# A two-block transformer forward pass on one core: neighbourhood heads in tiles of 128 queries with a shared turn of edge weights, and a last norm by square root

## The chip, the core and the metric

The kernel runs on one core of a Trainium2 chip. Five engines work from queues of their own: TensorE (PE in the profile, its weight loads PEld), VectorE (DVE), ScalarE (ACT), GpSimd (POOL) and SyncE (SP), which here only issues DMAs; ACT and POOL issue a few as well. The metric is device time in microseconds of one execution. Lower is better, and versions are compared by the median of several runs on the same chip.

## What is computed

The input is x, 256 tokens of width 1024, and two memories of 256 tokens. It passes through two blocks, all in float32. The first block has an even layer (global attention with rotary positions, window attention with a bias and a sink, memory attention, a gate) and an odd layer (neighbourhood attention with 16 heads of width 64, memory attention, a gate). The second block has a mixer (dilated attention and a short convolution), attention to a second memory, a squared-ReLU MLP of width 4096, and a last norm. The parts that matter here:

```python
def rmsnorm(x, g):
    y = xf * lax.rsqrt(jnp.mean(xf * xf, axis=-1, keepdims=True) + EPS)
    return y * g

def neighborhood_attn(q, k, v, rpb):      # a grid of 4 rows of 64 columns
    colmask = (col[None, :] >= cs[:, None]) & (col[None, :] < cs[:, None] + NA_COLS)
    def one(r):                           # the queries of one grid row
        s = einsum('bqhd,bikhd->bhqik', qblk, kblk) * scale + bias
        s = where(colmask[:, None, :], s, -inf)
        p = softmax(s.reshape(B, H, GRID_W, kr * GRID_W), axis=-1)
        return einsum('bhqik,bikhd->bqhd', p, vblk)
```

A query in grid column c sees 16 columns of all four rows: `cs = clip(c - 8, 0, 48)`. The output of the odd layer is multiplied by silu(gate) and projected; the second block ends with `rmsnorm(x, g_final_2)` after the MLP.

## The kernel before

**Precision.** A float32 operand is split into a high and a low part of type float32r (`split`, `hilo`): ACT writes the high part, DVE the rest. A projection is then three products, high-high, high-low and low-high, which accumulate in PSUM. Weights arrive by SP's DMAs in pieces of 1024 KB (tile `raw`, three buffers), are split into `wh` and `wl` (four buffers each) and multiplied; `wide` yields the pieces of a wide weight, and its `step` says how many k tiles of 128 rows one load holds.

**Order.** Nothing is issued while the program is built. Every operation is recorded by `Plan.record` (line 85) with its dependencies, and `Plan.solve` (line 262) orders all of them at once with a list scheduler: each engine takes, of the operations that are ready, the one with the smallest position in the program. The durations for that come from a cost model, `Plan.cost` (line 133). The order is then fixed and issued from line 286, which is why all instructions bear that line. Background work is queued by `later`, and `pace` lets a step of it in after every few matmuls of a projection (`RATE`); `flush` runs what is left of one tag. So the steps of attention heads lie between the matmuls of projections. Tiles of one tag share a number of buffers: `p` has `PB` = 4, `y` has `YB` = 5, `pp` has `PH` = 4, the large slots `SLOTS` = 24; PSUM has four banks tagged `at` and four tagged `mm`.

**The odd layer.** Its norm is done in `norm_later`, and `turns` transposes the result with TensorE. Here the tokens are put into the order of grid columns: token position = 4 * column + row, so that a query's neighbours lie close together (`by_column`). ACT and DVE do that when they read PSUM, through a strided view. Two groups of eight neighbourhood heads follow (`c0` and `c1`, loop at line 1253): keys, queries and values are projected, then `near_heads` (line 969) queues the steps of the heads.

**near_heads.** In column order, 128 queries see at most 160 keys (`SPAN`): queries 0 to 127 the keys 0 to 159, queries 128 to 255 the keys 96 to 255. `first` computes, for a head, the scores of both query tiles, adds the bias with DVE (which also finds the maximum), takes the exponential on ACT with its sum, and then copies, scaled by 1/sum, a part of 128 keys for each block of 64 queries: four operations on 64 partitions each, from key 0 or key 32 of the 160. Either DVE or ACT may do one (`scaled`, the planner chooses). `second` transposes the two 128x128 squares of a head on TensorE, and after both heads of a pair splits them into high and low (tile `pp`). `third` multiplies, for each of the four 64-query blocks b, a stationary value tile `v[b]` with the high and low weights of that block (128 moving columns), adds the high and low halves of the result with ACT and DVE and hands it to `gated`. The four value tiles hold the keys from 0, 32, 96 and 128 on (`NEAR`). The middle two are put together by POOL's DMAs from the outer two. `steps` (line 920) queues these: `second` of a head comes `LAG[0]` = 2 heads behind `first`, `third` of a pair one more behind. Behind a group's steps, `layer_odd` runs other projections and, after `flush`, the output projection (`out_proj`) of that group.

**The MLP.** It goes by slices of 512 hidden columns, `up` then `down`; the last `down_last` (line 1439) also does the last norm: sums of squares `ms` on ACT, their sum with EPS on DVE, the power -1/2 on POOL (line 1475), then scaling by DVE and ACT and the stores.

Of the kernel before, what the change touches and what calls it, by code (L numbers as in the profile page):

```python
# [16 lines left out]
P = 128  # L17
# [11 lines left out]
NEAR, SPAN = (0, 32, 96, 128), 160  # L29


class Plan:
# [100 lines left out]
    def cost(self, engine, method, args, kwargs, outs, ins):  # L133

        if method == "dma_start":
            o = outs[0]
            nbytes = 4 * math.prod(o.shape)
            return (1040.0 if engine == "gpsimd" else 50.0), 950.0, nbytes
        n = math.prod(outs[0].shape[1:])
        sbuf = not any(self.mine(v) and self.tiles[v.tensor.name]["pool"].space == bass.MemoryType.PSUM for v in ins)  # L140
        col = kwargs.get("bias") is not None or isinstance(kwargs.get("scale"), bass.AP)
        accum = kwargs.get("accum_out") is not None
        if engine == "tensor":
# [166 lines left out]
class Kernel:  # L310
# [347 lines left out]

    def turns(self, tag, halves, key, by_column=False):


        nc = self.nc
        rows, cols = (lambda v: v.rearrange("p (r c) -> p r c", c=COLS)), (lambda v: v.rearrange("p (c r) -> p r c", c=COLS))
        if not by_column:
            rows = cols = lambda v: v
# [303 lines left out]
    def near_heads(self, tag, gi, qs, ks, po, out, before):  # L969
# [4 lines left out]
        v = [self.slot([P, 4, 2, 2, 64], "vp") for _ in range(4)]  # L974
        for k, d in ((0, 0), (1, 3)):
            flat = v[d].rearrange("p r e l c -> p r (e l c)")
            h = bass.AP(flat.tensor, flat.offset, [list(flat.ap[0]), [256, 4], [192, 2], [1, 64]])
            l = bass.AP(flat.tensor, flat.offset + 64, [list(flat.ap[0]), [256, 4], [64, 2], [1, 64]])
# [5 lines left out]
        es, ps, ws = {}, {}, {}  # L984
        before()

        def first(h):
            r, e = divmod(h, 2)
            if e == 0:
# [5 lines left out]
                ps[r] = self.work("p", [P, 2, 2, P], PB)  # L995
            w, bias = ps[r][:, e], es.pop(h)
            st = self.work("st", [P, 8], 8)
            nmax, ssum = st[:, 0:2], st[:, 2:4]
            i, j = divmod(h, 4)
            sc = self.scores_stacked(qs[i][:, j, :], ks[i][0][:, j, :], ks[i][1][:, j, :], ((0, SPAN), (S - SPAN, SPAN)))  # L1000
            p = self.work("p", [P, 2, SPAN], PB)
# [12 lines left out]
        def second(h):  # L1014
            r, e = divmod(h, 2)
            if e == 0:
                ws[r] = self.psum("at", [P, 2, 2, P])
            pt = ws[r]
            for t in range(2):
                nc.tensor.transpose(pt[:, e, t, :], ps[r][:, e, t, :], self.ident)  # L1020
            if e == 1:
                w = self.work("pp", [P, 2, 2, 2, P], PH, F32R)
                self.hilo(w[:, 0], w[:, 1], pt)
                ws[r] = w.rearrange("p l e t (b q) -> p l e (t b) q", b=2)

        def third(r):
            w = ws.pop(r)
            u = self.work("y", [P, S], YB)
            o = self.work("y", [P, S], YB)
            blocks = lambda t: t.rearrange("p (b q) -> p b q", b=4)  # L1030
            for e in range(2):
                pv = self.psum("at", [P, 4, 2, 64])
# [4 lines left out]
                nc.scalar.activation(blocks(u[own]), pv[other, :, 0, :], AF.Copy)  # L1037
                nc.vector.tensor_tensor(blocks(u[own]), pv[own, :, 0, :], blocks(u[own]), ALU.add)
                nc.vector.tensor_tensor(blocks(o[own]), pv[own, :, 1, :], blocks(u[own]), ALU.add)
            out(r, o)  # L1040

        self.steps(tag, first, second, third, 8, 2)
# [348 lines left out]
    def mlp(self, ms):  # L1391
# [94 lines left out]
        def down(s, t):  # L1486
            for c in range(2):
                self.proj_n(self.wide(a["w_down_2"], 512 * s, 4, 512 * c), 4, 512, lambda l, k: t[l][:, k, :],
# [4 lines left out]
        for s in range(NS - 1):  # L1493
            t2 = up(s + 1)
# [37 lines left out]
YB = 5  # L1532
# [91 lines left out]
```

## Time and profile before

| | us |
|---|---|
| runs, median (lowest to highest of 3) | 774.47 (773.76 to 774.75) |
| the profiled execution | 772.73 |
| its span, first to last instruction | 770.8 |
| mean granted TensorE clock, share of full | 0.998 |

The span is a little shorter than the profiled execution's own time, because the latter includes what lies before the first and behind the last instruction. Stages in us from the span's start: the even layer to about 195, the odd layer's norm and projections, the neighbourhood heads of the first group from about 265 to 325 and of the second to 391, the mixer to 505, attention to the second memory to 590, the MLP to the end. The page first gives the busy time of each engine; other views give instructions in order of time, groups of equal instructions, and who waited for whom. In the timeline a row gives start and duration in us, engine, operation, tiles (out<-in), shape and count, and in brackets the idle time before it and what ended it; rows of groups give count, busy us, mean ns of one, and idle time before.

### The profile page before, as it was taken

How to read it: one execution, taken by the hardware profiler on the slowest of the kernel's cores; microseconds unless marked ns; L12 is line 12 of the kernel's file. 1: busy time of each engine (PE TensorE's matmuls, PEld its weight loads, DVE VectorE, ACT ScalarE, POOL GpSimd, SP SyncE). 2: the span in 40 equal slices, each digit the busy share in tenths (PEclk: the TensorE clock that was granted, in tenths of full speed). 3: DMA queues.
4: the chain of work that ended last, by engine and by line, in shares of the span. 5: the costliest groups of instructions: out<-in, count | busy, mean ns of one | idle time of the engine just before them, and what ended most of it. 6: DMA issues, size and time to landing. Idle time of an engine off the chain costs nothing.

```text
span 770.8 us, 11844 instructions
## 1 busy us (share of the span) xinstructions
PE 757.9 (98%) x4338; PEld 658.5 (85%) x4338; DVE 621.2 (81%) x1167; ACT 526.9 (68%) x1035; POOL 54.1 (7%) x90
## 2 busy tenths in 40 slices
PE   9999999999999999999999999999999999999996
PEld 7898888888888888788888888889988888888885
DVE  5999998998889889989998879887777665555565
ACT  5777986876679677766777778655656765555562
POOL 2240010000002201110001100100000000000000
PEclk9999999999999999999999999999999999999999
DMA  9893555454568975886356944375335665656541
GB/s 316 279 274 110 164 172 186 162 165 164 162 201 246 274 213 156 222 265 192 120 178 188 245 158 134 137 227 184 137 117 157 212 179 168 204 175 208 173 155 54
DMA packets 109785, 143.28 MB, mean 186 GB/s; under 512 B 3872, under 2 KB 80736, under 8 KB 109728
## 3 DMA queue, kind: packets, MB, share of 16 engines
q1 hardware_dynamic: 103184, 131.09, 52.4%
q0 software_dynamic: 6112, 11.01, 6.1%
q8 instruction: 34, 0.56, 0.3%
q10 hardware_dynamic: 432, 0.43, 0.2%
q14 instruction: 23, 0.19, 0.1%
HBM read 135.70 MB, written 1.05 MB: 177 GB/s over the span
## 4 chain that ended last, share of the span: by engine, by line
PE 79%; DVE 13%; DMA 3%; ACT 2%; issue 2%; SPq 1%; POOL 0%; POOLq 0%; DVEq 0%; ACTq 0%
PE t_mm L286 59%; PE t_at L286 20%; DVE t_wl L286 4%; DVE t_y L286 2%; DMA t_memT<-in_mem_t_dram 1%; DVE t_p L286 1%; DMA t_raw<-in_w_in_even_dram 1%; DVE t_x L286 1%; DMA t_xT<-in_x_t_dram 1%; DVE t_pp L286 1%; DVE t_st L286 1%; DVE t_sum L286 1%; ACT t_p L286 1%; SPq L286 1%; ACT t_wh L286 1%
## 5 line engine op out<-in xcount | busy, mean ns | idle before, releaser
L286 DVE TENSOR_TENSOR t_wl<-t_raw,t_wh 128x1024 fp32r<-128x1024 f32 (+2 forms) x238 | 287.8, 1214 | 63.6 <-ACT t_wh L286 60.7
L286 ACT ACTIVATE t_wh<-t_raw 128x1024 fp32r<-128x1024 f32 (+2 forms) x238 | 249.5, 1054 | 73.4 <-PE t_mm L286 56.0
L286 PE MATMUL t_mm<-t_mT,t_wh 128*128 128x512 f32 x496 | 180.4, 402 | 0.0
L286 PE MATMUL t_mm<-t_mT,t_wl 128*128 128x256 f32 x496 | 132.1, 285 | 0.0
L286 PE MATMUL t_mm<-t_wh,t_yh 128*128 128x512 f32 (+1 forms) x288 | 113.6, 394 | 0.0
L286 PE MATMUL t_mm<-t_wl,t_yh 128*128 128x512 f32 (+1 forms) x288 | 112.9, 392 | 0.0
L286 PE MATMUL t_mm<-t_wh,t_yl 128*128 128x512 f32 (+1 forms) x288 | 112.2, 392 | 0.0
L286 PEld LDWEIGHTS t_mm<-t_mT,t_wh 128*128 128x128 f32 x496 | 91.2, 188 | 13.8
L286 PEld LDWEIGHTS t_mm<-t_mT,t_wl 128*128 128x128 f32 x496 | 93.3, 189 | 6.4
L286 PE MATMUL t_at<-t_mT,t_wh 128*128 128x512 f32 x240 | 85.8, 395 | 0.0
L286 ACT COPY t_sum<-t_mm 128x256 f32<-128x256 f32 x90 | 33.3, 370 | 46.7 <-PE t_mm L286 45.9
L286 PE MATMUL t_mm<-t_wh,t_gh 128*128 128x256 f32 (+2 forms) x256 | 64.1, 334 | 0.0
L286 PEld LDWEIGHTS t_mm<-t_wl,t_yh 128*128 128x128 f32 x288 | 54.1, 188 | 11.0
L286 PEld LDWEIGHTS t_mm<-t_wh,t_yl 128*128 128x128 f32 x288 | 54.0, 188 | 11.0 <-DVE t_yl L286 0.2
L286 PEld LDWEIGHTS t_mm<-t_wh,t_yh 128*128 128x128 f32 x288 | 54.2, 188 | 10.7 <-ACT t_yh L286 0.4
L286 PE MATMUL t_at<-t_mT,t_wl 128*128 128x256 f32 x240 | 62.6, 280 | 0.0
L286 ACT ACTIVATE t_p<-t_p,t_st 128x256 f32<-128x256 f32 (+3 forms) x119 | 52.1, 454 | 11.5 <-DVE t_st L286 11.2
L286 PEld LDWEIGHTS t_at<-t_mT,t_wh 128*128 128x128 f32 x240 | 44.4, 188 | 8.2 <-issue 0.2
L286 PEld LDWEIGHTS t_at<-t_mT,t_wl 128*128 128x128 f32 x240 | 45.2, 188 | 3.6
L286 PE MATMUL t_mm<-t_hT,t_wh 128*128 128x512 f32 (+1 forms) x160 | 48.1, 356 | 0.0
L286 DVE TENSOR_TENSOR t_sum<-t_mm,t_sum 128x256 f32<-128x256 f32 x90 | 38.0, 422 | 11.9 <-ACT t_sum L286 10.6
L286 PEld LDWEIGHTS t_mm<-t_wh,t_gh 128*128 128x128 f32 x256 | 44.1, 191 | 3.6 <-ACT t_wh L286 0.4
(183 smaller groups left out, 1328.4 us busy)
## 6 DMA issues: line engine op xcount, KB each, us to landing
t_raw<-in_w_in_odd_dram SPq DMA_DIRECT2D x20, 1024.0 KB, 5.2
t_raw<-in_w_up_dram SPq DMA_DIRECT2D x16, 1024.0 KB, 5.8
t_raw<-in_w_down_dram SPq DMA_DIRECT2D x16, 1024.0 KB, 5.2
t_raw<-in_w_in_dram SPq DMA_DIRECT2D x12, 1024.0 KB, 5.4
t_raw<-in_w_in_even_dram SPq DMA_DIRECT2D x10, 1024.0 KB, 5.1
t_raw<-in_w_mem_kv_dram SPq DMA_DIRECT2D x8, 1024.0 KB, 5.1
t_raw<-in_w_out_even_dram SPq DMA_DIRECT2D x6, 1024.0 KB, 5.0
t_raw<-in_w_out_odd_dram SPq DMA_DIRECT2D x6, 1024.0 KB, 5.0
```

Source lines behind the costliest of these rows:

```text
L286: f(*[self.real(v) for v in args], **{k: self.real(v) for k, v in kwargs.items()})
```

## The change

- **near_heads** works by tiles of 128 queries. Each tile has its own 128 keys (queries 0 to 127: keys 0 to 127; the others: keys 128 to 255) and 32 edge keys (128 to 159, or 96 to 127). There are two value tiles, and one small tile `edges` with edge keys of the values, which POOL's DMAs place at partitions 32 j for head j of a four.
- `first` scales the own part in place, full width, and writes the edge part, 32 keys for each of two tiles, into a tile shared by four heads (`rests`).
- `second` transposes the own parts of a pair. A new step `turn_rest` transposes the edge parts of four heads at once, keeps the 64 queries of each tile that see edge keys, and splits them.
- `third` has, for each query tile, one matmul over 128 keys (256 moving columns) and one over 32 edge keys (128 moving columns) that adds to half of it.
- The steps are queued by a list of positions instead of `steps`; `third` of both pairs of four heads follows their `turn_rest`. `YB` is 6.
- **turns**: with `by_column`, the transposes write PSUM in column order, and ACT and DVE read it contiguously.
- **Last norm**: square root on ACT and reciprocal on DVE instead of the power on POOL; for the second token tile the last sum goes in as the root's bias. A root on two values is taken early in the MLP, in the pass s = 1.
- **Loads**: the down weights of the last two slices come in halves of 512 KB.
- **Cost model**: a matmul costs at least 111 ns (before, (at least 128 columns)/2.4 + 13.3 = 66.6); ACT work on fewer than 128 partitions costs 100 ns more, DVE work 84 ns more.

```diff
-            return 108.0 if method == "transpose" else max(n * slow, 128) / 2.4 + 13.3, 0.0, 0
+            return 108.0 if method == "transpose" else max(n * slow / 2.4 + 13.3, 111.0), 0.0, 0
-            return n / 1.2 + (93 if sbuf else 51) + 94 * col + 93 * accum + self.table, 0.0, 0
+            return n / 1.2 + (93 if sbuf else 51) + 94 * col + 93 * accum + 100 * half + self.table, 0.0, 0
-            return n / 0.96 + 68 + 62 * ptr + 82 * accum, 0.0, 0
+            return n / 0.96 + 68 + 62 * ptr + 82 * accum + 84 * half, 0.0, 0
...
+    def by_column(v, t):
+        return v.rearrange("p (c r) -> p r c", c=COLS)[:, 2 * t:2 * t + 2, :]
...
-                    nc.tensor.transpose(pt[:, j, t * P:(t + 1) * P], halves[c][:, t, k * P:(k + 1) * P], self.ident)
+                    nc.tensor.transpose(place(pt[:, j, :], t), halves[c][:, t, k * P:(k + 1) * P], self.ident)
-                h, l, v = cols(f(0, 4 * c + k)), cols(f(1, 4 * c + k)), rows(pt[:, j, :])
+                h, l, v = f(0, 4 * c + k), f(1, 4 * c + k), pt[:, j, :]
...
-        for d in (1, 2):
-            n = P - NEAR[d]
-            nc.gpsimd.dma_start(v[d][:n], v[0][NEAR[d]:])
-            nc.gpsimd.dma_start(v[d][n:], v[3][:P - n])
+        edges = self.slot([P, 2, 2, P], "ve")
+        for t, at in enumerate(AT):
+            for j in range(4):
+                if EDGE * j != at:
+                    nc.gpsimd.dma_start(edges[EDGE * j:EDGE * j + EDGE, t], v[1 - t][at:at + EDGE, :, j]
+                                        .rearrange("p i l c -> p i (l c)"))
...
+            edge = bass.AP(p.tensor, p.offset + P, [list(p.ap[0]), [EDGE, 2], [1, EDGE]])
+            nc.vector.tensor_tensor(rests[i][:, :, j, :], edge, ssum.unsqueeze(2).to_broadcast([P, 2, EDGE]), ALU.mult)
             for t in range(2):
-                for b in range(2):
-                    rows, k0 = slice(64 * b, 64 * b + 64), 32 * b
-                    self.scaled(w[rows, t, :], p[rows, t, k0:k0 + P], ssum[rows, t:t + 1])
+                main = p[:, t, EDGE * t:EDGE * t + P]
+                self.scaled(main, main, ssum[:, t:t + 1])
...
+        def turn_rest(i):
+            rest = rests[i]
+            pt = self.psum("at", [P, 2, P])
             for t in range(2):
+                nc.tensor.transpose(pt[:, t, :], rest[:, t].rearrange("p j k -> p (j k)"), self.ident)
+            w = rests[i] = self.work("y", [P, 2, 2, 64], YB, F32R)
+            seen = bass.AP(pt.tensor, pt.offset + 64, [list(pt.ap[0]), [64, 2], [1, 64]])
+            self.hilo(w[:, 0], w[:, 1], seen)
...
-                for b in range(4):
-                    nc.tensor.matmul(pv[:, b], v[b][:, r, e].rearrange("p l c -> p (l c)"), w[:, :, e, b, :],
-                                     start=True, stop=True)
+                for t in range(2):
+                    main, edge = stationary(h, t)
+                    qs_ = slice(64 - 64 * t, 128 - 64 * t)
+                    nc.tensor.matmul(pv[:, t], main, w[:, :, e, t, :], start=True, stop=False)
+                    nc.tensor.matmul(pv[:, t, :, qs_], edge, rest[rows, :, t, :], start=False, stop=True)
...
-        self.steps(tag, first, second, third, 8, 2)
+        steps = [(h, lambda h=h: first(h)) for h in range(8)]
+        steps += [(2 * r + 1.2 + LAG[0], lambda r=r: second(r)) for r in range(4)]
+        steps += [(4 * i + 3.3 + LAG[0], lambda i=i: turn_rest(i)) for i in range(2)]
+        steps += [(4 * (r // 2) + r % 2 + 3.4 + LAG[0] + LAG[1], lambda r=r: third(r)) for r in range(4)]
...
-            parts = [list(self.wide(a["w_down_2"], 512 * s, 4, 512 * c)) for c in range(2)]
+            parts = [list(self.wide(a["w_down_2"], 512 * s, 4, 512 * c, step=2)) for c in range(2)]
...
                 if tt == 1:
-                    nc.vector.tensor_tensor(r, r, ms[:, 2:3], ALU.add)
-                nc.gpsimd.tensor_tensor(r, r, self.mhalf[:, :1], ALU.pow)
+                    nc.scalar.activation(r, ms[:, 2:3], AF.Sqrt, bias=r)
+                else:
+                    nc.scalar.activation(r, r, AF.Sqrt)
+                nc.vector.reciprocal(r, r)
...
+            if s == 1:
+                nc.table = 1300.0
+                nc.scalar.activation(self.work("st", [P, 8], 8)[:, :2], r2, AF.Sqrt)
+                nc.table = 0.0
...
-YB = 5
+YB = 6
```

More of the change, by code (lines that the diff above doesn't have):

```diff
@@ L142, in cost @@
         accum = kwargs.get("accum_out") is not None
+        half = outs[0].shape[0] < P
         if engine == "tensor":
@@ L657, in square_sum @@
                          "op1": ALU.add, "accum_out": ms}))
+    @staticmethod
+    def by_column(v, t):
+        return v.rearrange("p (c r) -> p r c", c=COLS)[:, 2 * t:2 * t + 2, :]
     def turns(self, tag, halves, key, by_column=False):
         nc = self.nc
[L663 to L665 removed]
+        place = self.by_column if by_column else lambda v, t: v[:, t * P:(t + 1) * P]
         f = Halves(lambda: self.slot([P, 2, 2, S], "mT"))
@@ L994, in first @@
                 es[h], es[h + 1] = near[:, 0], near[:, 1]
-                ps[r] = self.work("p", [P, 2, 2, P], PB)
-            w, bias = ps[r][:, e], es.pop(h)
+            if j == 0:
+                rests[i] = self.work("y", [P, 2, 4, EDGE], YB)
+            bias = es.pop(h)
             st = self.work("st", [P, 8], 8)
             nmax, ssum = st[:, 0:2], st[:, 2:4]
-            i, j = divmod(h, 4)
             sc = self.scores_stacked(qs[i][:, j, :], ks[i][0][:, j, :], ks[i][1][:, j, :], ((0, SPAN), (S - SPAN, SPAN)))
-            p = self.work("p", [P, 2, SPAN], PB)
+            p = ps[h] = self.work("p", [P, 2, SPAN], PB)
             for t in range(2):
@@ new lines, in second @@
+        def second(r):
+            pt = self.psum("at", [P, 2, 2, P])
+            for e in range(2):
+                p = ps.pop(2 * r + e)
+                for t in range(2):
+                    nc.tensor.transpose(pt[:, e, t, :], p[:, t, EDGE * t:EDGE * t + P], self.ident)
+            w = ws[r] = self.work("pp", [P, 2, 2, 2, P], PH, F32R)
+            self.hilo(w[:, 0], w[:, 1], pt)
+        def turn_rest(i):
+            rest = rests[i]
+            pt = self.psum("at", [P, 2, P])
+            for t in range(2):
+                nc.tensor.transpose(pt[:, t, :], rest[:, t].rearrange("p j k -> p (j k)"), self.ident)
+            w = rests[i] = self.work("y", [P, 2, 2, 64], YB, F32R)
+            seen = bass.AP(pt.tensor, pt.offset + 64, [list(pt.ap[0]), [64, 2], [1, 64]])
+            self.hilo(w[:, 0], w[:, 1], seen)
@@ L1036, in third @@
                 own, other = slice(64 * e, 64 * e + 64), slice(64 - 64 * e, 128 - 64 * e)
-                nc.scalar.activation(blocks(u[own]), pv[other, :, 0, :], AF.Copy)
-                nc.vector.tensor_tensor(blocks(u[own]), pv[own, :, 0, :], blocks(u[own]), ALU.add)
-                nc.vector.tensor_tensor(blocks(o[own]), pv[own, :, 1, :], blocks(u[own]), ALU.add)
+                nc.scalar.activation(halves(u[own]), pv[other, :, 0, :], AF.Copy)
+                nc.vector.tensor_tensor(halves(u[own]), pv[own, :, 0, :], halves(u[own]), ALU.add)
@@ L1045, in rope @@
+        for _, step in sorted(steps, key=lambda s: s[0]):
+            self.later(tag, step)
     def rope(self, tag, po, n, i, rx):
```

47 lines of the change are left out of this document (24 added, 23 removed).

## The prediction, made before the changed kernel ran

> **What bounds the kernel now.** First the page's busy line and the chain that ended last.
>
> ```profile
> span 770.8 us, 11844 instructions
> PE 757.9 (98%) x4338; PEld 658.5 (85%) x4338; DVE 621.2 (81%) x1167; ACT 526.9 (68%) x1035; POOL 54.1 (7%) x90
> PE 79%; DVE 13%; DMA 3%; ACT 2%; issue 2%; SPq 1%; POOL 0%; POOLq 0%; DVEq 0%; ACTq 0%
> ```
>
> TensorE is the bound: matmuls cover 757.9 of 770.8 us. So time can fall in three ways only: fewer matmul slots, fewer waits of TensorE inside, or a shorter tail behind the last matmul. Work taken from VectorE (DVE) or ScalarE (ACT) counts only where TensorE waits for it. Next the busy time of the first neighbourhood stage, and what the weight loads (PEld) waited for between 255 and 410 us, where both groups of neighbourhood heads lie.
>
> ```profile
> 255.00:325.00 70.00, 68.83 (x387) 59.05 (x387) 63.51 (x139) 51.46 (x106) 10.79 (x18) 1.00 0.75 212
> ...
> PEld t_at L286 <- ACT t_sum L286: 2.0, 3, 1.4
> PEld t_at L286 <- ACT t_wh L286: 0.8, 2, 0.6
> PEld t_at L286 <- DVE t_xg L286: 0.7, 1, 0.7
> ...
> PEld t_at L286 <- ACT t_p L286: 0.3, 1, 0.3
> ```
>
> The columns of the first row are length, then busy us of PE, PEld, DVE, ACT and POOL, then the granted clock (1.00) and DMA. The t_xg wait belongs to the norm behind the stage; the other six, 3.1 us, stand in front of the neighbourhood's product of weights and values (t_at<-t_pp,t_vp). The longest, in the timeline:
>
> ```profile
> 318.86 1.39 DVE L286 TENSOR_TENSOR t_ks<-t_sum,t_ks 64x512 fp32r<-64x512 f32 x2
> ...
> 320.96 0.68 DVE L286 TENSOR_TENSOR t_pp<-t_at,t_pp 128x512 fp32r<-128x512 f32 x1
> ...
> 321.76 0.97 PEld L286 LDWEIGHTS t_at<-t_pp,t_vp 128*128 128x128 f32 x8 [1.41 <-ACT t_sum L286]
> 321.79 1.08 PE L286 MATMUL t_at<-t_pp,t_vp 128*128 128x128 f32 x8 [1.12 <-DVE t_pp L286]
> ```
>
> PE names the true releaser: the low half of the turned weights, t_pp, which came late because DVE had a queue ahead of it (the k stack until 320.25). The weight load had waited 1.41 us and the array stood idle for 1.12, so some 0.29 us was covered by the matmul in flight. For six waits I take 0.13 of cover each: 3.1 - 0.8 = 2.3 us is what the near stage can give back.
>
> **Prices of matmul slots.** From TensorE's timeline:
>
> ```profile
> 284.88 0.48 PE L286 MATMUL t_mm<-t_wl,t_yh 128*128 128x512 f32 x1
> 285.20 0.27 PE L286 MATMUL t_at<-t_cst,t_p 128*128 128x128 f32 x1
> 285.23 0.48 PE L286 MATMUL t_mm<-t_wh,t_yl 128*128 128x512 f32 x1
> 285.54 0.56 PE L286 MATMUL t_at<-t_pp,t_vp 128*128 128x128 f32 x4
> 285.94 0.44 PE L286 MATMUL t_mm<-t_wh,t_yh 128*128 128x512 f32 x1
> ...
> 760.27 0.39 PE L286 MATMUL t_mm<-t_wh,t_yl 128*128 128x512 f32 x1
> 760.50 0.28 PE L286 MATMUL t_mm<-t_wh,t_yh 128*128 128x256 f32 x1
> 760.62 0.28 PE L286 MATMUL t_mm<-t_wl,t_yh 128*128 128x256 f32 x1
> ```
>
> Starts count, since the ends are modelled. 512 columns take 0.23 us (760.27 to 760.50), 256 take 0.12 (760.50 to 760.62). 512 columns and a transpose take 0.35 (284.88 to 285.23): a transpose is 0.12. 512 columns and four products of 128 columns take 0.71 (285.23 to 285.94): (0.71 - 0.23)/4 = 0.12 each. 128 columns cost as much as 256; a slot has a floor of about 0.12, where half of the 256 columns' time would be 0.06.
>
> **The change, part by part.**
>
> *Product with the values.* Before: four matmuls of 128 columns a head, 4 x 0.12 = 0.48 us. After: two of 256 columns (own keys) and two of 128 columns over 32 rows (edge keys): 2 x 0.12 + 2 x 0.12 = 0.48. Over 16 heads 0.0. Every matmul in this trace reads 128*128, so the 32-row form is not shown. Below, an edge could cost 0.06: 32 x 0.06 = 1.9 us less. Above, see the second rival. I take 0.12, the nearest row.
>
> *Transposes.* Two a head as before, and two more for each four heads' edges: 8 x 0.12 = **+1.0 us** on the bound engine.
>
> *DVE and ACT in the stage.*
>
> ```profile
> L286 DVE TENSOR_SCALAR t_p<-t_p,t_st 64x128 f32<-64x128 f32 x42 | 11.1, 285 | 0.8
> L286 ACT ACTIVATE t_p<-t_p,t_st 64x128 f32<-64x128 f32 x22 | 8.2, 396 | 4.1 <-DVE t_st L286 4.0
> L286 DVE TENSOR_SCALAR t_p<-t_p,t_st 128x128 f32<-128x128 f32 x5 | 1.4, 285 | 0.1
> L286 DVE TENSOR_TENSOR t_tanh<-t_p,t_ropetab 128x32 f32<-128x32 f32 x8 | 1.0, 186 | 0.0
> L286 DVE TENSOR_TENSOR t_pp<-t_at,t_pp 128x128 fp32r<-128x128 f32 x8 | 2.2, 278 | 0.0
> L286 ACT ACTIVATE t_pp<-t_at 128x128 fp32r<-128x128 f32 x8 | 2.2, 280 | 0.0
> ```
>
> The 64 half-width scalings (42 + 22, four a head) cost 19.3 us. A full-width one costs DVE the same 285 ns, so 32 of them cost half, 9.7. Added: 16 products of 64 columns for the edges, between 186 (32 columns) and 278 (128 columns), 0.21 taken, 3.4 us; and four splits of turned edges, 4 x (0.28 + 0.28) = 2.2. Net 19.3 - 9.7 - 3.4 - 2.2 = 4.0 us off two engines in some 130 us. Both had gaps, so it counts only at the six waits. Besides, the third step of the second pair of each four no longer runs ahead of the last t_pp: its DVE work moves behind it. The tail of a group in step order becomes second, edge turn, third, third, where it was second, third directly. So t_pp has three steps before its product instead of one. I take three quarters of 2.3: **-1.7 us**. Bounds: 0 and -2.3. What is late next: the edge turn, on which both last thirds of a group now hang.
>
> *Values, edges and their DMAs.*
>
> ```profile
> L286 POOL DMA_DIRECT2D t_vp<-t_vp x8 | 4.1, 518 | 17.4 <-DVE t_vp L286 17.4
> ...
> t_raw<-in_w_down_dram SPq DMA_DIRECT2D x16, 1024.0 KB, 5.2
> ...
> t_raw<-in_w_kv_mem_dram SPq DMA_DIRECT2D x8, 512.0 KB, 3.4
> ```
>
> POOL issues 12 small copies instead of 8: 4 x 0.52 = 2.1 us more on an engine that is busy 7%; behind them wait the loads of the bias tables (t_near). The gate projection lies between copies and first use. Cost 0. The last down projections load halves: 512 KB land in 3.4 us against 5.2, four more than before on SP. Half a load feeds two k tiles, 12 matmuls, 12 x 0.23 = 2.7 us, and three buffers hold 8 us of it, over 3.4. Cost 0; without that cover a gap would be below 3.4 - 2.7 = 0.7 us a load.
>
> *Transposes by column.* ACT's rows at the odd layer's norm, against those of two later norms:
>
> ```profile
> L286 ACT ACTIVATE t_mT<-t_at,t_gT 128x256 fp32r<-128x256 f32 x8 | 4.1, 708 | 0.7 <-PE t_at L286 0.7
> ...
> L286 ACT ACTIVATE t_mT<-t_at,t_gT 128x256 fp32r<-128x256 f32 x16 | 6.3, 483 | 0.5 <-PE t_at L286 0.3
> ```
>
> Reading in order saves ACT 8 x 0.22 = 1.8 us; the value projection covers that norm, no wait of TensorE stands there, so 0. The 16 transposes now write with a step; at worst each doubles, 16 x 0.12 = +1.9; 0 taken, since nothing but their destination differs.
>
> *Last norm.* The end of the kernel:
>
> ```profile
> 764.47 0.19 ACT L286 ACTIVATION_READ_ACCUMULATOR t_p<-t_x 128x1 f32 x1
> 764.69 0.16 DVE L286 TENSOR_TENSOR t_rstd<-t_rstd,t_ms 128x1 f32<-128x1 f32 x1 [0.18 <-ACT t_p L286]
> 764.99 0.56 POOL L286 TENSOR_TENSOR t_rstd<-t_rstd,t_mhalf 128x1 f32<-128x1 f32 x1 [4.61 <-DVE t_rstd L286]
> 765.58 0.68 DVE L286 TENSOR_SCALAR t_xg<-t_xg,t_rstd 128x512 f32<-128x512 f32 x2 [0.73 <-POOL t_rstd L286]
> ...
> L286 ACT ACTIVATE t_st<-t_st,t_sink 128x2 f32<-128x2 f32 x8 | 2.3, 288 | 0.0
> ...
> L286 ACT ACT_TABLE_LOAD x1 | 1.3, 1283 | 1.7 <-PEq L1608 1.7
> ```
>
> From 764.66 to 765.58 are 0.92 us by DVE and POOL. After: a root on ACT at once, with a column as bias (0.29, as the sink's row), then a reciprocal on DVE as short as the 0.16 of the addition, and two hand-overs of 0.03: 0.51. **-0.4 us**, all on the path. The early root in the MLP loads its table once, 1.28 us on an ACT that idles between splits there; cost 0, on the path at worst +1.3.
>
> *The written order.* The planner now prices a matmul at 111 ns at least and adds 84 to 100 ns to half-width work; the whole kernel is ordered anew, also where no operation changes. What that can move are waits such as the early ones (20 to 255 us):
>
> ```profile
> PEld t_at L286 <- DVE t_p L286: 1.6, 2, 1.0
> PEld t_at L286 <- ACT t_p L286: 1.4, 5, 0.4
> ```
>
> The 111 is near the 0.12 measured, the 64-partition rows above do cost what 128 partitions cost, so the plan is truer; I take a quarter of these 3.0, **-0.8**, with -2.5 and +2.5 as bounds.
>
> **Sum.** 0.0 + 1.0 - 1.7 - 0.4 - 0.8 = -1.9 us. The profiled execution took 772.73 us (770.8 its span, 1.9 around it): 770.8 after. The median of the runs shown is 774.47, so 772.6. About 0.2% (1.5 us) is what a measurement can tell from no change here; the forecast is just beyond it.
>
> **Rivals.** *The wait moves (0.28).* Both last thirds of a group hang on one edge turn that needs all four heads; TensorE then waits before them, or before the output projection. For it: DVE is busy 63.5 of 70 us in that stage. Against: 4 us less work there. Without the -1.7: -0.2, 774.3 us, no change.
>
> *The array empties between 128-row and 32-row work (0.10, slower).* Each head has four such borders (own, edge, own, edge), 64 in all. A 512-column record lasts 0.39 us and the next starts after 0.23; if the 0.16 between is lost at each border, 64 x 0.16 = 10.2 us, 782.8. It turns the change slower from (1.5 + 1.9)/64 = 0.05 us a border. No row shows a border of this kind, for or against. The Trainium skill, "TensorEngine Tiling (Array Packing)", section Tiling Modes, says that changing the tiling mode drains the engine; its page "TensorE: Matmul & The Clock Gate" says that one 32-row matmul takes as long as a 128-row one, and by that the sum stays as above.
>
> *The new order is worse (0.10), +4.5 on the forecast:* the early waits rise by 2.5 and the near ones stay: 777.1, slower. *Or better (0.08):* early waits fall by 2.5 and edges cost 0.06 to 0.12: near 769.5.
>
> *The root's table is changed back and forth (0.03, slower):* four loads of 1.28 us around the two roots, three of them on the path: -1.9 + 3.8 = +1.9, 776.4.
>
> **How the numbers follow.** Forecast 0.41. Faster: 0.41 + 0.08 = 0.49; no change 0.28; slower 0.10 + 0.10 + 0.03 = 0.23. Range: below, all bounds of gain, -1.9 + 1.0 - 2.3 - 0.4 - 2.5 = -6.1, 768.4; above, +1.0 + 2.5 = +3.5, 778.0. It leaves out the emptying array (0.10) and the ends of the others.
>
> **What would show it.** Product groups t_at<-t_pp with starts 0.12 apart (more than 0.2 at each change of rows: second rival); PEld's waits before them below 1.4 us in all; eight more t_at<-t_cst transposes; the tail from last accumulator to scaling near 0.5 us; one more ACT_TABLE_LOAD only. Wrong would make it: new waits at the edge turn or at the output projections, or early waits that grow.

## The result: slower by 0.9%, and the profile after

The changed kernel took 780.73 us (median of four runs, 780.17 to 781.68) beside 774.12 for the kernel before on the same chip (four runs): a ratio of 1.0088, with an interval of 1.0071 to 1.0106. The forecast was 772.6 us, in a range from 768.4 to 778.0, with slower at 0.23. The time lies outside the range, beyond its upper end, and within 2.1 us of the 782.8 that the second rival (the array empties, chance 0.10) gave. The profiled execution took 780.75 us, its span 778.9.

The page of the changed kernel, its busy line and the chain that ended last:

```profile
span 778.9 us, 11875 instructions
PE 767.6 (99%) x4346; PEld 664.1 (85%) x4346; DVE 617.9 (79%) x1166; ACT 523.3 (67%) x1033; POOL 54.0 (7%) x92
PE 87%; DVE 7%; DMA 3%; ACT 1%; issue 1%; SPq 1%; POOL 0%; DVEq 0%; ACTq 0%; POOLq 0%
```

DVE and ACT are busy for a little less, as the change means it, and of the chain more belongs to TensorE (87% where it was 79%). PE is busy for 9.7 us more (767.6 beside 757.9) with only 8 matmuls more. So the loss is inside TensorE's own time, and not in a wait for another engine. The next view divides the span into stretches. Its row for the stretch with both groups of neighbourhood heads, first of the kernel before:

```profile
255.00:415.00 160.00, 158.02 (x914) 136.67 (x914) 147.03 (x318) 117.95 (x247) 17.23 (x28) 1.00 0.67 197
```

and of the changed kernel:

```profile
255.00:415.00 160.00, 159.85 (x856) 134.02 (x854) 135.42 (x299) 107.26 (x228) 18.72 (x31) 0.99 0.60 178
```

The second number is PE's busy time, the one in brackets its matmuls. TensorE looks busier than before (159.85 of 160 us), and yet it starts 58 matmuls fewer in the same time (856 beside 914). "Busy" is no measure of speed here: the lost time stands inside records that overlap, and only the starts show it. TensorE's timeline of the changed kernel, in a run of products with the values:

```profile
312.97 0.40 PE L287 MATMUL t_mm<-t_mT,t_wh 128*128 128x512 f32 x1
313.30 0.32 PE L287 MATMUL t_at<-t_y,t_vp 32*128 32x128 f32 x1
313.55 0.39 PE L287 MATMUL t_at<-t_pp,t_vp 128*128 128x256 f32 x1
...
315.01 0.32 PE L287 MATMUL t_at<-t_y,t_ve 32*128 32x128 f32 x1
315.26 0.38 PE L287 MATMUL t_at<-t_pp,t_vp 128*128 128x256 f32 x1
315.57 0.32 PE L287 MATMUL t_at<-t_y,t_ve 32*128 32x128 f32 x1
315.82 0.38 PE L287 MATMUL t_at<-t_pp,t_vp 128*128 128x256 f32 x1
316.14 0.32 PE L287 MATMUL t_at<-t_y,t_vp 32*128 32x128 f32 x1
316.39 0.38 PE L287 MATMUL t_mm<-t_mT,t_wl 128*128 128x256 f32 x1
316.61 0.39 PE L287 MATMUL t_mm<-t_mT,t_wh 128*128 128x512 f32 x1
...
317.50 1.05 PE L287 MATMUL t_mm<-t_mT,t_wh 128*128 128x512 f32 x2
318.35 0.41 PE L287 MATMUL t_mm<-t_mT,t_wl 128*128 128x256 f32 x1
318.56 0.63 PE L287 MATMUL t_mm<-t_mT,t_wh 128*128 128x512 f32 x1
318.99 0.41 PE L287 MATMUL t_mm<-t_mT,t_wl 128*128 128x256 f32 x1
319.20 0.63 PE L287 MATMUL t_mm<-t_mT,t_wh 128*128 128x512 f32 x1
```

No row has idle time in front of it. From an own product (128*128, 128 rows) to the next edge product (32*128, 32 rows) are 0.31 to 0.32 us (315.26 to 315.57, 315.82 to 316.14), from an edge to the next own 0.25 (315.01 to 315.26, 315.57 to 315.82). The forecast had 0.12 for each. A pair takes 0.57 instead of 0.24, so a change of rows (a border) costs (0.57 - 0.24)/2 = 0.165 us. The rival had priced it at 0.16 from the overlap of two records. The first border of a run looks cheaper: 0.33 us from the 512-column product to the edge (312.97 to 313.30), 0.10 over the slot of 0.23. The rest comes behind the run, where the first full-height product takes 0.10 more than its slot (0.22 for 256 columns, 316.39 to 316.61). In the order of starts the changed kernel has 56 borders and not the 64 of the code, because the planner orders the matmuls anew and some edges follow one another. What the starts at these borders lie apart beyond the slot of the matmul in front (0.12, or 0.23 for 512 columns) comes to 8.0 us, and the 0.10 behind each of eleven runs to 1.2: 9.2 us together, which is 56 x 0.165.

The last rows show a second thing: from 317.5 us on the same matmuls take about twice as long (512 columns 0.43, from 318.56 to 318.99, instead of 0.23). The stretches around it, where the number behind POOL's is the granted clock:

```profile
310.00:317.50 7.50, 7.50 (x40) 5.73 (x39) 6.87 (x12) 4.58 (x10) 1.31 (x2) 0.99 0.93 261
317.50:321.00 3.50, 3.50 (x13) 2.98 (x13) 2.15 (x4) 1.43 (x2) 0.89 (x2) 0.53 1.07 376
```

For 3.4 us, less than a microsecond behind the run of borders, the clock was halved, which is 1.7 us of lost work in this execution. The profiled execution of the kernel before has no such stretch before its last matmul. The other runs of the changed kernel have mean clocks from 0.993 to 0.998, so this loss need not be the same in each.

Much of what had been predicted of the other parts did appear. Groups of equal instructions of the changed kernel, with count, busy us and mean ns:

```profile
L287 DVE TENSOR_TENSOR t_y<-t_p,t_st 128x64 f32<-128x64 f32 x16 | 3.3, 220 | 0.2
...
L287 ACT ACTIVATE t_mT<-t_at,t_gT 128x256 fp32r<-128x256 f32 x8 | 3.0, 490 | 0.7 <-PE t_at L287 0.7
...
L287 ACT ACT_TABLE_LOAD x2 | 2.6, 1283 | 1.7 <-PEq L1645 1.7
...
L287 PE MATMUL t_at<-t_cst,t_y 128*128 128x128 f32 x8 | 1.8, 272 | 0.0
```

The edge products on DVE take 220 ns (0.21 predicted), ACT's reads at the odd layer's norm 490 instead of 708, one more table load, eight more transposes. The tail, in order of time:

```profile
773.98 0.19 ACT L287 ACTIVATION_READ_ACCUMULATOR t_p<-t_x 128x1 f32 x1
774.20 0.29 ACT L287 ACTIVATE t_rstd<-t_ms,t_rstd 128x1 f32<-128x1 f32 x1
774.52 0.16 DVE L287 RECIPROCAL t_rstd<-t_rstd 128x1 f32<-128x1 f32 x1 [0.50 <-ACT t_rstd L287]
774.72 0.68 DVE L287 TENSOR_SCALAR t_xg<-t_xg,t_rstd 128x512 f32<-128x512 f32 x2
```

From the accumulator's end (774.17) to the scaling are 0.55 us where 0.92 were: the 0.4 of the forecast. And what the weight loads waited for between 255 and 415 us (total, times, longest):

```profile
PEld t_at L287 <- issue: 1.5, 6, 0.3
PEld t_at L287 <- ACT t_wh L287: 0.5, 2, 0.2
PEld t_at L287 <- DVE t_wl L287: 0.2, 1, 0.2
```

No wait for t_sum or t_p is left. The nine waits that remain all stand in front of the weight load of an edge product, 0.24 to 0.25 us each, so they belong to the borders, whatever engine the view names. So the waits of the forecast are gone, and the tail and the prices of DVE and ACT went as forecast; what was put at zero, the form of the products, took more than all of it. What removed the waits is another question, which the experiments below answer differently from the forecast.

### The profile page after: what moved, and what is told of

It reads as the page before. It is cut to its first block, busy times and chain, and to the rows that moved or that the text cites. A ratio compares the mean times of both kernels' runs of the same rounds, so it can differ in the third digit from the quotient of the medians.

```text
span 778.9 us, 11875 instructions
## 1 busy us (share of the span) xinstructions
PE 767.6 (99%) x4346; PEld 664.1 (85%) x4346; DVE 617.9 (79%) x1166; ACT 523.3 (67%) x1033; POOL 54.0 (7%) x92
## 4 chain that ended last, share of the span: by engine, by line
PE 87%; DVE 7%; DMA 3%; ACT 1%; issue 1%; SPq 1%; POOL 0%; DVEq 0%; ACTq 0%; POOLq 0%
PE t_mm L287 64%; PE t_at L287 23%; DVE t_wl L287 2%; DMA t_memT<-in_mem_t_dram 1%; DMA t_raw<-in_w_in_even_dram 1%; DMA t_xT<-in_x_t_dram 1%; DVE t_p L287 1%; DVE t_x L287 1%; SPq L287 1%; DVE t_xg L287 1%; DVE t_xs L287 0%; ACT t_p L287 0%; DVE t_qs L287 0%; DVE t_y L287 0%; POOL t_rstd L287 0%
## 5 line engine op out<-in xcount | busy, mean ns | idle before, releaser
L287 ACT ACTIVATE t_p<-t_p,t_st 128x256 f32<-128x256 f32 (+2 forms) x113 | 49.1, 454 | 8.7 <-DVE t_st L287 8.5
```

The lines of the kernel that those rows point to most:

```text
L287: f(*[self.real(v) for v in args], **{k: self.real(v) for k, v in kwargs.items()})
```

## Experiments

Theory A: the array empties at each change between 128-row and 32-row products, and all else in the change is a small gain. Theory B: the edge product is slow because it adds to a PSUM region that was only just written (accumulation). Theory C: the new order of the whole kernel is worse. Theory D: a 32-row product is dear in itself, wherever it stands. The texts on record before each run call them 'border', 'accumulate', 'order' and 'row'.

### Fewer borders, the same products

The products of a pair of heads are grouped: four own ones, then four edges.

```diff
+            pvs = [self.psum("at", [P, 2, 2, P]) for _ in range(2)]
+            for e in range(2):
+                for t in range(2):
+                    nc.tensor.matmul(pvs[e][:, t], stationary(2 * r + e, t)[0], w[:, :, e, t, :], start=t == 0, stop=False)
             for e in range(2):
...
                 for t in range(2):
...
-                    nc.tensor.matmul(pv[:, t], main, w[:, :, e, t, :], start=True, stop=False)
-                    nc.tensor.matmul(pv[:, t, :, qs_], edge, rest[rows, :, t, :], start=False, stop=True)
+                    nc.tensor.matmul(pvs[e][:, t, :, qs_], stationary(h, t)[1], rest[rows, :, t, :], start=False, stop=t == 1)
...
```

> The changed kernel, with the edge products of a pair of heads grouped: four own products of 128 rows first, then four edge products of 32 rows (before: own, edge, own, edge). Same matmuls, 16 borders between row counts instead of 64. In the trace of the changed kernel a border costs 0.165 us (own to edge 0.32 us from start to start, edge to own 0.25, against 0.12 each), 64 of them 10.6 us, and a stretch of 3.4 us at half clock, 1.7 us, follows the longest run of them. Theory 'border': 48 x 0.165 = 7.9 us less, and the half-clock stretch gone: 771 to 773 us. Rival 'row' (a product over 32 rows is dear in itself, wherever it stands, because its weights can't be loaded ahead): an edge behind an edge still takes 0.25 or more, 779 to 781 us. Rival 'order' (the 6.6 us come from the new order of the rest): 780 us.

Measured: 772.16 us, ratio 0.999 (0.998 to 0.9999) to the kernel before. Its order of starts has 22 borders where the changed kernel has 56, and summed as above they cost 3.3 us instead of 9.2. Its timeline:

```profile
309.80 0.32 PE L287 MATMUL t_at<-t_y,t_vp 32*128 32x128 f32 x1
309.80 0.43 PE L287 MATMUL t_at<-t_y,t_ve 32*128 32x128 f32 x3
310.17 0.50 PE L287 MATMUL t_at<-t_pp,t_vp 128*128 128x256 f32 x2
310.60 0.43 PE L287 MATMUL t_at<-t_y,t_ve 32*128 32x128 f32 x3
310.76 0.27 PE L287 MATMUL t_at<-t_y,t_vp 32*128 32x128 f32 x1
310.96 0.39 PE L287 MATMUL t_mm<-t_mT,t_wl 128*128 128x256 f32 x1
```

Ten products from 309.80 to 310.96, 0.116 us each with three borders among them, where the changed kernel needs 0.57 for two. Two edge products of different heads, which lie in different groups of 32 rows, start within the same hundredth of a microsecond (309.80 and 309.80); the other two of the pair follow 0.16 later (310.60 to 310.76). Most of the loss is gone with the borders, although all products, sums and sizes stayed. D falls with this: four edge products in a row take 0.37 us (309.80 to 310.17), less than four slots of 0.12. C does not fit: the cost model and all other parts are those of the changed kernel, though the planner made a new order here too.

The same trace shows that the width of the product in front does not set the price. Where 512-column products alternate with edges one by one, from such a product to the edge are 0.43 us (358.95 to 359.38), 0.20 over its slot and as dear as behind 256 columns.

### No border, the same sums

Edge products over all 128 rows: the small value tile of a head is filled with zeros outside its 32 rows.

```diff
-        edges = self.slot([P, 2, 2, P], "ve")
+        edges = [self.slot([P, 2, 4, P], "ve") for _ in range(2)]
         for t, at in enumerate(AT):
+            nc.gpsimd.memset(edges[t].bitcast(F32), 0.0)
             for j in range(4):
-                if EDGE * j != at:
...
-                    nc.tensor.matmul(pv[:, t, :, qs_], edge, rest[rows, :, t, :], start=False, stop=True)
+                    nc.tensor.matmul(pv[:, t, :, qs_], edge, rest[:, :, t, :], start=False, stop=True)
```

> The changed kernel, with every edge product over 128 rows: the edge values of each head stand in a tile of their own with zeros in the other heads' rows, so the same turned edge weights of four heads can be the moving side. Same number, order and columns of matmuls, same accumulation into the same bank, no border at all. Added: four fills with zeros on GpSimd, four more small copies. Theory 'border' and rival 'row' alike: all 10.6 + 1.7 us go, 768 to 769.5 us. Rival 'accumulate' (an edge waits because it adds to what the own product has just written): own to edge stays at 0.32 us, 780 us. Rival 'order': 780 us.

Measured: 770.11 us, ratio 0.9958 (0.9943 to 0.9973); 0.6 above the upper end expected, and far below what B or C need. Its timeline:

```profile
311.86 0.23 PE L287 MATMUL t_at<-t_y,t_ve 128*128 128x128 f32 x1
311.92 0.34 PE L287 MATMUL t_at<-t_pp,t_vp 128*128 128x256 f32 x1
312.09 0.23 PE L287 MATMUL t_at<-t_y,t_ve 128*128 128x128 f32 x1
312.15 0.33 PE L287 MATMUL t_at<-t_pp,t_vp 128*128 128x256 f32 x1
312.32 0.22 PE L287 MATMUL t_at<-t_y,t_ve 128*128 128x128 f32 x1
```

The same pair of own and edge product, with the same accumulation, takes 0.23 us (311.86 to 312.09) instead of 0.57. B falls: a full-height edge product that adds to the same place costs nothing beyond its slot. Four times the rows, three quarters of them zeros, are cheaper than the change of rows. Against the changed kernel the difference is 10.6 us between the two medians, and 9.6 when each is taken against the kernel before of its own runs (780.73 - 774.12 = 6.6 more and 773.14 - 770.11 = 3.0 less). The traces account for 10.4: 9.2 for the borders and 1.7 for the stretch at half clock, which does not occur here, less 0.5 because in the changed kernel four pairs of edges start together (4 x 0.12).

### Eight and eight

Both pairs of a four together: eight own products, then eight edges. The loops are those of the first experiment over four heads, and the last step takes both pairs:

```diff
-        steps += [(4 * (r // 2) + r % 2 + 3.4 + LAG[0] + LAG[1], lambda r=r: third(r)) for r in range(4)]
+        steps += [(4 * i + 3.4 + LAG[0] + LAG[1], lambda i=i: third(i)) for i in range(2)]
```

> The changed kernel with the products of four heads together: eight own products, then eight edge products of 32 rows; 8 borders in all, where the changed kernel has 64 and the pairs had 16. Theory 'border', with 0.165 us a border and grouped edges at some 0.06 us each as the trace of the pairs shows: 1.3 us for borders against 2.6, so 770.5 to 771.5 us, and near the padded kernel (770.1). Rival: the four PSUM banks that it holds at once make TensorE wait: above 772.2 us.

Measured: 770.81 us, ratio 0.9973 (0.9962 to 0.9984), as expected. Its order has 10 borders, which cost 1.4 us by the same count. So 56, 22 and 10 borders give ratios of 1.0088, 0.999 and 0.9973 to the kernel before. The padded kernel with none is at 0.9958, though edges that start together should make the grouped ones cheaper than it; what they lose elsewhere was not traced, and the intervals of the two (0.9962 to 0.9984 and 0.9943 to 0.9973) overlap.

### The two halves of the change

The changed kernel with the old near_heads (all its steps, tiles and copies), the rest of the change kept:

```diff
-        v = [self.slot([P, 2, 4, 2, 64], "vp") for _ in range(2)]
+        v = [self.slot([P, 4, 2, 2, 64], "vp") for _ in range(4)]
...
-                    nc.tensor.matmul(pv[:, t], main, w[:, :, e, t, :], start=True, stop=False)
-                    nc.tensor.matmul(pv[:, t, :, qs_], edge, rest[rows, :, t, :], start=False, stop=True)
+                    nc.tensor.matmul(pv[:, b], v[b][:, r, e].rearrange("p l c -> p (l c)"), w[:, :, e, b, :],
+                                     start=True, stop=True)
```

> The changed kernel with the neighbourhood heads as they were before (64-query blocks, four value tiles), and all else of the change kept: cost model, transposes by column, last norm by root, half loads, six y buffers. Theories 'border' and 'row': the loss lies in the heads, so 774.1 - 0.4 (tail) with up to 1 us either way from the new order: 773 to 774.5 us. Rival 'order': near 780 us.

Measured: 769.18 us, ratio 0.9944 (0.993 to 0.9959). The expectation (773 to 774.5) missed by 4 us: the rest of the change was thought to be worth little beyond the tail, and gives 4.0 us. This is the lowest median of all that ran, but the interval overlaps those of the padded kernel above and of two versions below (the cost model alone, and the power back).

The kernel before with the new near_heads alone, so the reverse of that diff, and

```diff
-YB = 5
+YB = 6
```

> The kernel before with only the new neighbourhood heads and six y buffers; cost model, transposes by column, last norm and loads as before. Theories 'border' and 'row': the loss is all here, plus the tail's 0.4 us: 780.5 to 782 us. Rival 'order' (the changed cost model): near 774 us.

Measured: 783.25 us, ratio 1.0127 (1.0111 to 1.0144), 1.3 us above the upper end of what was expected. Its order has 54 borders, which cost 9.2 us counted as above. It also has two stretches at half clock, one at 14.5 us and one right behind a run of borders:

```profile
383.00:386.60 3.60, 3.60 (x19) 2.43 (x19) 3.54 (x7) 2.43 (x6) 0.00 (x0) 1.00 0.17 39
386.60:390.10 3.50, 3.50 (x13) 3.02 (x12) 1.35 (x4) 1.20 (x3) 0.00 (x0) 0.51 0.34 115
```

The second one costs 1.7 us (3.5 at a clock of 0.51). Whether the first explains the 1.3 us was not tried.

### The parts of the rest, one at a time on the kernel before

The cost model alone:

```diff
+        half = outs[0].shape[0] < P
...
-            return 108.0 if method == "transpose" else max(n * slow, 128) / 2.4 + 13.3, 0.0, 0
+            return 108.0 if method == "transpose" else max(n * slow / 2.4 + 13.3, 111.0), 0.0, 0
...
-            return n / 1.2 + (93 if sbuf else 51) + 94 * col + 93 * accum + self.table, 0.0, 0
+            return n / 1.2 + (93 if sbuf else 51) + 94 * col + 93 * accum + 100 * half + self.table, 0.0, 0
...
-            return n / 0.96 + 68 + 62 * ptr + 82 * accum, 0.0, 0
+            return n / 0.96 + 68 + 62 * ptr + 82 * accum + 84 * half, 0.0, 0
```

> The kernel before with the new cost model alone (matmuls 111 ns at least, half-width work dearer); the operations are the same, only their order changes. Theory 'truer plan': the rest of the 4.0 us, some 2 us, is order: 770.5 to 772 us, with fewer waits of the weight loads before the neighbourhood products. Rival: the order's effect is chance or nothing, 772.5 to 774 us.

Measured: 770.05 us beside 772.79, ratio 0.996 (0.9947 to 0.9973). Not one operation differs, and 2.7 us are gone, a little more than expected. Its waits of the weight loads between 255 and 415 us:

```profile
PEld t_at L287 <- issue: 0.7, 3, 0.3
PEld t_at L287 <- DVE t_pp L287: 0.5, 1, 0.5
PEld t_mm L287 <- DVE t_yl L287: 0.4, 1, 0.4
PEld t_at L287 <- DVE t_xg L287: 0.3, 1, 0.3
```

and the row of that stretch:

```profile
255.00:415.00 160.00, 159.61 (x926) 138.58 (x925) 146.26 (x313) 120.88 (x254) 15.47 (x26) 1.00 0.68 202
```

With the old heads the waits for t_sum (2.0 us) and t_wh (0.8) are gone, and TensorE idles for 0.4 us in this stretch where it idled for 2.0 (160 - 159.61 and 160 - 158.02). The forecast had given these waits to the new heads; a plan with truer prices removes them without. This is one order that the planner found; no other set of prices was tried.

Root in place of the power, alone:

```diff
                 if tt == 1:
-                    nc.vector.tensor_tensor(r, r, ms[:, 2:3], ALU.add)
-                nc.gpsimd.tensor_tensor(r, r, self.mhalf[:, :1], ALU.pow)
+                    nc.scalar.activation(r, ms[:, 2:3], AF.Sqrt, bias=r)
+                else:
+                    nc.scalar.activation(r, r, AF.Sqrt)
+                nc.vector.reciprocal(r, r)
...
+                nc.scalar.activation(self.work("st", [P, 8], 8)[:, :2], r2, AF.Sqrt)
...
```

> The kernel before with the last norm by root and reciprocal alone (and the early root that loads its table). The changed kernel with the old heads runs 4.0 us below the kernel before, more than the 1.2 us that the prediction gave the parts outside the heads; its span from the last matmul's start to the end is 6.1 us, before 7.6. Theory 'closing': besides the 0.4 us of the shorter chain, GpSimd no longer computes last; before, its closing DRAIN came behind the power, took 5.09 us and ended at 770.06, 0.9 us behind SyncE's own, so some 1.3 to 1.4 us go: 771.6 to 772.0 us. Rival: only the chain counts, 0.4 us: 772.7 us; the table load of 1.28 us could take it back.

Measured: 772.93 us, ratio 0.9996 (0.9985 to 1.0006): nothing that can be measured, where 1.3 to 1.4 us were expected. In its trace the end is shorter indeed (6.4 us from the last matmul's start, 7.6 before), but the last matmul starts 1.7 us later (764.9 beside 763.3). The reverse, the version with the old near_heads but with the power back:

```diff
...
-                    nc.scalar.activation(r, r, AF.Sqrt)
-                nc.vector.reciprocal(r, r)
...
+                nc.gpsimd.tensor_tensor(r, r, self.mhalf[:, :1], ALU.pow)
...
-                nc.scalar.activation(self.work("st", [P, 8], 8)[:, :2], r2, AF.Sqrt)
```

> The changed kernel with the old heads (the run at 769.18 us, 0.9944 of the kernel before), and also the old last norm by GpSimd's power, no early root. Of that run's 4.0 us the cost model alone gave 2.7, the root alone nothing that could be measured, though its span from the last matmul on was 1.2 us shorter. Theory 'closing' (the shorter end is worth its 1.2 to 1.5 us): 0.996 of the kernel before, as with the cost model alone, 770 to 770.8 us. Rival (the end's gain is lost elsewhere): 0.9944, 769 to 769.5 us.

Measured: 769.44 us, ratio 0.9952 (0.9937 to 0.9967), beside 0.9944 (0.993 to 0.9959) with the root. The intervals overlap nearly whole. What the root is worth lies between 0 and about 1 us and stays open.

The transposes by column alone:

```diff
-                    nc.tensor.transpose(pt[:, j, t * P:(t + 1) * P], halves[c][:, t, k * P:(k + 1) * P], self.ident)
+                    nc.tensor.transpose(place(pt[:, j, :], t), halves[c][:, t, k * P:(k + 1) * P], self.ident)
...
-                h, l, v = cols(f(0, 4 * c + k)), cols(f(1, 4 * c + k)), rows(pt[:, j, :])
+                h, l, v = f(0, 4 * c + k), f(1, 4 * c + k), pt[:, j, :]
```

> The kernel before with the transposes that write in column order alone. Prediction: nothing, 773.1 us, since TensorE has no wait in that norm; ACT's eight reads there fall from 708 to about 490 ns. Rival: a stepped write to PSUM doubles 16 transposes, 775 us.

Measured: 772.41 us, ratio 0.9995 (0.9986 to 1.0005). And the loads in halves alone:

```diff
-            parts = [list(self.wide(a["w_down_2"], 512 * s, 4, 512 * c)) for c in range(2)]
+            parts = [list(self.wide(a["w_down_2"], 512 * s, 4, 512 * c, step=2)) for c in range(2)]
...
-                self.proj_n(self.wide(a["w_down_2"], 512 * s, 4, 512 * c), 4, 512, lambda l, k: t[l][:, k, :],
+                self.proj_n(self.wide(a["w_down_2"], 512 * s, 4, 512 * c, step=2 if s == NS - 2 else 4), 4, 512, lambda l, k: t[l][:, k, :],
```

> The kernel before with the last two slices' down weights in halves alone. Prediction: nothing, 773.1 us. Rival: a part of the 4.0 us, because pieces are split earlier: up to 1 us less; or three buffers hold too little: up to 1 us more.

Measured: 772.8 us, ratio 0.9997 (0.9987 to 1.0007). Neither does anything that can be measured, as forecast for both.

## Why the prediction was wrong

**The step that failed** is "Product with the values", with the sentence "I take 0.12, the nearest row". The nearest row was a product of 128 columns over 128 rows among its like, and nothing in the trace of before showed a product over 32 rows, or one beside another height. The 56 borders came to 9.2 us, and the half clock behind some of them to 1.7 in the profiled execution, where the term stood at 0.0. The bound above was known and priced: 0.16 at each of 64 borders, 10.2 us, 782.8. Measured were 0.165 a border, and 780.73. The price of a border was right; that the whole time came so near is in part luck, for the rival counted eight borders too many and no half clock. It was given a chance of 0.10 because no row spoke for or against it, and the range left it out.

The Trainium skill, "TensorEngine Tiling (Array Packing)", section Tiling Modes, has the rule that a change of the tiling mode drains the engine. The traces agree that each change costs time, and put a number to it: 0.165 us a change between products of 256 columns over 128 rows and of 128 columns over 32. That the engine empties meanwhile is no row of a trace. The Trainium skill, "TensorE: Matmul & The Clock Gate", section "Why this matters for your kernels", says that a single 32-row matmul takes as long as a 128-row one and that the gain lies in tiles running at the same time. The first half stood in the prediction as the case against the rival; it speaks of one kind of product by itself, and is silent on the alternation. The second half agrees with the grouped kernel, where edges of different heads start together.

**Transposes, +1.0.** In line with the runs: the padded kernel, without borders, stands 0.9 us above the version with the old near_heads (770.11 and 769.18), and these eight transposes are TensorE's extra work in it. The intervals of the two overlap, so the size is not shown, but nothing speaks for more.

**Near-stage waits, -1.7, and the written order, -0.8.** The sum, -2.5, was nearly right (-2.7 measured for the cost model alone), but by luck: its split was wrong. The waits went by the new order, with the old heads in place. So the new heads had nothing left to give. The row of the version with the old near_heads for the stretch from 255 to 415 us

```profile
255.00:415.00 160.00, 159.55 (x927) 138.55 (x926) 146.66 (x315) 121.28 (x256) 16.72 (x28) 1.00 0.67 200
```

against that of the padded kernel

```profile
255.00:415.00 160.00, 159.03 (x928) 138.93 (x927) 143.74 (x315) 115.80 (x245) 23.51 (x39) 1.00 0.64 189
```

shows the relief that was forecast for DVE and ACT (2.9 and 5.5 us here, where 4.0 were predicted for the two together) and no less idle time of TensorE: 0.45 us in the one and 0.97 in the other, the latter in front of the norm behind the heads. TensorE was hardly waiting for the heads any more.

**Tail, -0.4.** Its chain is 0.4 us shorter in the trace, as worked out; in the runs it cannot be told from nothing.

**Columns, halves, copies, table: 0.** Nothing was measured for the first two when made alone. Copies were not tried by themselves, and the table load only together with the root; the rest as a whole gains, and the rival with the table changed back and forth did not occur (two loads in all).

**The other rivals.** "The wait moves" did not occur: no wait at the edge turn or at the output projections is in the trace. "The new order is worse" does not fit the cost model alone, which is 2.7 us faster. Its sum has a slip besides: waits that rise by 2.5 instead of falling by 0.8, and 1.7 that stay, are +5.0 and not +4.5.

In sum: without the new near_heads the change gives 4.0 us, with them in a form without borders 3.0, and the borders with what follows them take back some 10. Of the 4.0, 2.7 are the cost model's. What makes up the rest was not settled, since no other part shows anything by itself and the intervals of the two (0.993 to 0.9959 and 0.9947 to 0.9973) overlap.

## What to carry to other kernels

Products over 32 rows among full-height ones on TensorE cost about 0.16 us at each change here, part of which shows only in the first start behind them: group them, so that there are few changes, or fill them up with zeros, which here was at least as cheap. A planner's prices are worth correcting before its kernel is rewritten, as the 2.7 us here show, and a forecast that hangs on a form no row shows should keep its range open to the dear end. Where the bounding engine is 99% busy, compare how many instructions it starts in a stretch, not its busy share.

## What was not expected of the hardware

- **Half clock in a busy stretch.** In the profiled execution of the changed kernel the clock fell to half for 3.4 us shortly behind a run of borders, and likewise in the kernel with the new near_heads alone at 386.6 us; in the kernels with fewer or no borders it did not before the last matmul. PE counts as busy without a gap in front of it (7.50 of 7.50 us). The Trainium skill, "TensorE: Matmul & The Clock Gate", Part 1, says that the clock is halved after an idle window of about 3.4 us and released after a busy one; the length agrees, an idle window of that length is not in the records. That the emptied array counts as idle would fit, and was not tried. A similar run of borders at 384.5 us in the changed kernel had no such stretch behind it, and the traces offer a reason: the clock changes in each lie whole multiples of 3.413 us apart. On that grid the run at 313 us lies mostly in one window (313.94 to 317.35, eight borders), while the run at 384.5 us is cut at 385.62. In both kernels the window in front of the late halving streams the fewest columns of all windows with borders: 3712 where the next has 4096, and 3328 where the next has 3840.
- **POOL's closing drain.** In the kernel before, the instructions at the end of the program include a drain on POOL of 5.09 us, behind the power (count, then min, median and max in ns):

```profile
L1620 POOLq DRAIN  x3: 51/98/5087, 765.0 to 770.6; - x3
```

  In the version with the old near_heads and the root it takes 5.26 us, but it starts at 591.2 us, long before the end:

```profile
L1631 POOLq DRAIN  x3: 51/98/5258, 591.2 to 767.3; - x3
```

  From the last matmul's start to the end of the span are 7.6 us in the kernel before and 6.1 in that version. The times do not show this gain of 1.5 us. In both pairs of traces with and without the root the last matmul starts later with it (764.9 beside 763.3 us, and 761.5 beside 760.5 with the old near_heads and the new prices), so 1.7 us are lost where 1.2 are gained at the end, and 1.0 where 1.5 are. Single executions of one kernel differ by about as much, so why stays open.
